# Where the causal mask of a prompt's attention scores is added: by TensorE products or by VectorE

## The chip, the cores and the metric

The kernel runs on one core of a Trainium2 chip. A core has TensorE (PE, matrix products into PSUM), VectorE (DVE), ScalarE (ACT), GpSimd (POOL), and SyncE (SP), which here only issues DMAs. The metric is the device time of one execution in microseconds (us); lower is better. Three executions before the change took 427.47, 427.66 and 428.17 us.

## The reference

One layer of a decoder is computed for a prompt of 256 tokens and for 8 sequences of 4 new tokens each (288 tokens in all, model width 1024). An input projection gives two groups of mixers. One is a gated spatial mixer (4 groups of 128 channels). The other is attention with 8 heads of 64: the new tokens attend to a paged cache of 1024 old tokens by blocks, and the prompt attends to itself, causally, inside one block of 256 keys. Then come an output projection, an MLP of width 4096 and a gated per-layer embedding. What matters here is the prompt's attention:

```python
mask = slot_ok[None, None, :, :, None] & (pos <= t[None, None, :, None, None])
s = jnp.einsum('bhqd,bhqnkd->bhqnk', q, kg).astype(jnp.float32) * (d ** -0.5)
s = jnp.where(mask, s, -jnp.inf)
p = jax.nn.softmax(s.reshape(b, h, nq, -1), axis=-1)
```

## The kernel before

Activations lie with features on the partitions and 288 tokens along the free axis. Weights are streamed in 104 chunks of 512 KB: a DMA on SP's queue brings `raw`, ACT writes its rounded half `hi` (L132), DVE the rest `lo` (L139), and every product is three passes on TensorE (L221, L222, L223). Cached pages of 256 KB come in 16 tiles of 8 pages (`kvt`, four buffers, L160), eight tiles of keys and eight of values; they are asked for on the queues of SP, POOL and ACT.

The first part of the program follows the string `ORDER`: `w` is a chunk of weights, `T` a tile of pages (`u_K`, products at L543; `u_V`, L615), `G` a group of the spatial mixer (`u_g`, L458, L460), `A` a pair of heads of the prompt's attention (`u_A`), `P` the load of the embedding's input (`load_p`, L310). There are four `A`. Units are generators, so that a later part of a unit runs some turns later, after other work. The order of an engine's queue is not simply that of the text: the framework puts the instructions of each engine in order by its own estimates of when each can run, apart from those kept in program order. After this part come the MLP's 64 chunks and the gate's 8.

`u_A(j)` for one pair of heads works in this order. Scores of each head go into one PSUM bank of the ring `misc` (3 banks), for the first 128 queries against 128 keys and for the second 128 against 256 keys (L480; the two heads use rows 0 to 63 and 64 to 127 of the array). To each of the four blocks on the diagonal, a product of an identity with a mask of 0 and -1e30 is added in PSUM (L483). DVE then takes the row maxima from PSUM (L494, L495) and scales them (L496). ACT takes Exp from PSUM into `P` with the row sums (L498, L500). DVE inverts the sums (L503) and scales `P` (L505, L506). TensorE transposes `P` through a third bank (L516), ACT and DVE copy the result to SBUF (L520, L518), TensorE multiplies with the values (L527), and the result is split into two halves (L227, L228). The identity and the mask of the products are a rounded copy `mask_r` of two 128x128 blocks of `const`, made once by ACT (L667).

Of the kernel before, what the change touches and what calls it, by code (L numbers as in the profile page):

```python
# [8 lines left out]
F32R = mybir.dt.float32r  # L9
I32 = mybir.dt.int32  # L10
AF = mybir.ActivationFunctionType
OP = mybir.AluOpType
AX = mybir.AxisListType
# [6 lines left out]
SCALE = 0.125  # L20
NEG = -1e30
# [14 lines left out]

# w: next chunk of weights, T: next tile of cached pages, G: group of the spatial gate, A: head pair of the prompt's
# attention, m: masks, P: input of the layer embedding, s and S: stores, -: a turn without matrix products of its own
ORDER = (
# [6 lines left out]
def tile_decode_step(ctx: ExitStack, tc: tile.TileContext, w, xT, pT, kT, vP, pt, vec, const, aws, abd, abs_,  # L46
                     y_o, k_o, vp_o, vs_o, s_o):
    nc = tc.nc
    pe, act, dve, pool, sp = nc.tensor, nc.scalar, nc.vector, nc.gpsimd, nc.sync
# [5 lines left out]
    def stile(shape, tag, bufs=1, dt=F32):  # L55
        uid[0] += 1
        return sb.tile(shape, dt, name=f"{tag}_{uid[0]}", tag=tag, bufs=bufs)
# [16 lines left out]

# [1 line left out]
    pt_sb = stile([1, 64], "pt", dt=I32)  # L76
    vec_sb = stile([128, 38], "vec")
    cst = stile([128, 476], "const")
    aws_sb = stile([128, 4, 128], "aws")
# [3 lines left out]
    eps = stile([128, 1], "eps")  # L83
# [4 lines left out]
    first = stile([128, 1], "first")  # L88
# [10 lines left out]
    ident = cst[:, 0:128]  # L99
    cmask = cst[:, 128:256]  # L100
    blk = cst[:, 256:384]
    omask = cst[:, 384:448]
    hmask = cst[:, 448:456]
    sel = cst[:, 456:472]
    iota = cst[:, 472:476]

# [1 line left out]
    h = stile([128, 8, N], "h")  # L108
# [5 lines left out]

# [1 line left out]
    NW = w.shape[0]  # L116
# [25 lines left out]

    # pages are asked for at the pace of the arithmetic, so that weights don't queue behind them
    pace = {"pe": 0.0, "dma": 0.0, "page": 0, "used": 0, "w": 6, "split": 2, "wn": 0}
# [18 lines left out]

# [1 line left out]
    pending = []  # L165
# [14 lines left out]
    def step(unit=None, weights=None, us=2.95):  # L180
        """One turn of the pipeline. A generator that yields n goes on n turns later, with those that read PSUM;
        n + 0.5: with those that need PE, after them; 0: at the end of this turn."""
        if weights is not None:
            pace["wn"] = weights
            for c in range(pace["split"], weights + 1):
                load_w(c)
                split_hi(c)
                split_lo(c)
                pace["split"] = c + 1
        ahead = [c for c in range(pace["split"], pace["wn"] + 3) if c in raw]  # L190
        for c in ahead:
            split_hi(c)
            pace["split"] = c + 1
        for q in pending:
            q[0] = max(q[0] - 1, 0)
        due(0)
        due(1)
        if unit is not None:
            resume(unit)
        for c in ahead:  # L200
            split_lo(c)
        # the second half of w_out waits for the last page
        for c in range(pace["w"], pace["split"] + NRAW):
            if c in raw or c >= NW:
                pace["w"] = c + 1
            elif c < W_HOLD or pace["page"] >= PAGE_HOLD:
                load_w(c)
                pace["w"] = c + 1
                pace["dma"] += 1.46
            else:  # L210
                break
        load_pages(us)
        due(2)
# [4 lines left out]

# [1 line left out]
    def mm3(out, wh, wl, xh, xl, start, stop):  # L220
# [17 lines left out]
    def rsqrt_act(ss, count):  # L238
        """first guess of 1/sqrt(ss/count + eps), its square, and -(ss/count + eps)/2"""
        y, v, y2 = tmp(), tmp(), tmp()  # L240
        act.activation(y, ss, AF.Abs_reciprocal_sqrt, bias=eps, scale=1.0 / count)
        act.activation(v, ss, AF.Identity, bias=heps, scale=-0.5 / count)
        act.activation(y2, y, AF.Square)
        return y, v, y2
# [19 lines left out]

# [1 line left out]
    def load_x(i):  # L266
# [38 lines left out]

# [1 line left out]
    def load_p():  # L307
# [55 lines left out]

# [1 line left out]
    def in_tile(c, name, tag):  # L365
# [27 lines left out]
    def nat(src, dst_p, dst_s):  # L393
        """src [128 feat, 288 tokens] -> dst_p [128 tokens, 2, 128 feat], dst_s [32 tokens, 128 feat]"""
        p = misc_ps()
        for c in range(2):
            pe.transpose(p[:, 128 * c:128 * c + 128], src[:, 128 * c:128 * c + 128], ident)  # L397
        pe.transpose(p[0:NS, 256:384], src[:, NP:N], ident)
        act.activation(dst_p, p[:, 0:256].rearrange("p (c f) -> p c f", c=2), AF.Copy)
        act.activation(dst_s, p[0:NS, 256:384], AF.Copy)  # L400
# [51 lines left out]

# [1 line left out]
    def u_g(g):  # L454
# [17 lines left out]

# [1 line left out]
    def u_A(j):  # L474
        qn, kn = st["q"], st["k"]
        S = [misc_ps(), misc_ps()]
        for q0, c0, n in ((0, 0, 128), (128, 256, 256)):
            for hh in range(2):
                pp = slice(64 * hh, 64 * hh + 64)
                pe.matmul(S[hh][:, c0:c0 + n], lhsT=qn[pp, j, q0:q0 + 128], rhs=kn[pp, j, 0:n], start=True, stop=False,  # L480
                          tile_position=(64 * hh, 0))
            for hh in range(2):
                pe.matmul(S[hh][:, c0 + n - 128:c0 + n], lhsT=mask_r[:, 0:128], rhs=mask_r[:, 128:256],  # L483
                          start=False, stop=True)
        yield 1
# [7 lines left out]
        for hh in range(2):  # L493
            dve.tensor_reduce(mx[:, 2 * hh:2 * hh + 1], S[hh][:, 0:128], AX.X, OP.max)  # L494
            dve.tensor_reduce(mx[:, 2 * hh + 1:2 * hh + 2], S[hh][:, 256:512], AX.X, OP.max)  # L495
        dve.tensor_scalar(mx, mx, -SCALE, None, op0=OP.mult)  # L496
        for hh in range(2):
            act.activation(P[hh][:, 0:128], S[hh][:, 0:128], AF.Exp, bias=mx[:, 2 * hh:2 * hh + 1], scale=SCALE,  # L498
                           accum_out=sm[:, 2 * hh:2 * hh + 1])
            act.activation(P[hh][:, 128:384], S[hh][:, 256:512], AF.Exp, bias=mx[:, 2 * hh + 1:2 * hh + 2],  # L500
                           scale=SCALE, accum_out=sm[:, 2 * hh + 1:2 * hh + 2])
# [29 lines left out]

# [1 line left out]
    def u_K(t):  # L533
# [98 lines left out]

# [1 line left out]
    def u_out(c, half, i):  # L634
# [27 lines left out]

# [1 line left out]
    mask_r = stile([128, 256], "maskr", dt=F32R)  # L664

    def mask_aws():
        act.activation(mask_r, cst[:, 0:256], AF.Copy)  # L667
        tc.keep_in_program_order(pool.dma_start(aws_sb, aws))
        tc.keep_in_program_order(pool.dma_start(abd_sb, abd))
        tc.keep_in_program_order(pool.dma_start(abs_sb, abs_.partition_broadcast(128)))  # L670
        pool.affine_select(out=aws_sb, in_=aws_sb, pattern=[[0, 4], [1, 128]], compare_op=OP.is_ge, fill=0.0, base=0,
                           channel_multiplier=-1)
        pool.affine_select(out=abd_sb, in_=abd_sb, pattern=[[0, 4], [1, NS]], compare_op=OP.is_ge, fill=0.0, base=0,
                           channel_multiplier=-1)
# [36 lines left out]

# [1 line left out]
    hid = []  # L713
# [3 lines left out]
    for nm in ("T5", "T6"):  # L717
        t = stile([128, 4 * N], nm)
# [74 lines left out]
def _constants():  # L793
    import numpy as np
    c = np.zeros((128, 476), np.float32)
    i = np.arange(128)
    c[:, 0:128] = np.eye(128)
    c[:, 128:256] = np.where(i[None, :] <= i[:, None], 0.0, NEG)
    c[:, 256:384] = (i[:, None] // 64 == i[None, :] // 64)
    b4, q = i // 32, (i % 32) // 8  # L800
    for g in range(2):
        key = np.arange(32)
        ok = (key[None, :] // 4 == (4 * g + b4)[:, None]) & (key[None, :] % 4 <= q[:, None])
        c[:, 384 + 32 * g:416 + 32 * g] = np.where(ok, 0.0, NEG)
    c[:, 448:456] = (i[:, None] % 8 == np.arange(8)[None, :])
    c[:, 456:472] = (i[:, None] // 8 == np.arange(16)[None, :])
    c[:, 472:476] = np.arange(1, 5)[None, :]
    return c
# [56 lines left out]
```

## Time and profile before

| | before |
|---|---|
| time, three executions | 427.47, 427.66, 428.17 us |
| profiled execution: span from first to last instruction | 425.1 us |
| what lies around the span, if the profiled execution took the median | 2.6 us |
| TensorE busy | 414.2 us (97%) |
| VectorE busy | 270.0 us (64%) |
| ScalarE busy | 206.9 us (49%) |
| mean granted TensorE clock, share of full | 0.995 |

Busy time of TensorE counts each product to its modelled end, and these ends overlap the next product, so 97% does not say that the array streams all the time. The chain that ended last, followed back from the last instruction, says which engine's work the end waited for.

### The profile page before, as it was taken

To read this page: it belongs to the slowest core of one execution; us is meant where nothing else is said; L and a number is where in the kernel's file an instruction comes from. 1 tells how busy PE (TensorE), PEld (TensorE's weight loads), DVE (VectorE), ACT (ScalarE), POOL (GpSimd) and SP (SyncE) were. 2 spreads that over 40 slices of the span, in tenths; PEclk is the share of its full clock that TensorE was granted. 3 is DMA by queue.
4 is the path that set the end of the run, shared out by engine and by line. 5 is a ranking of instruction groups with operands and counts; after the bars stand their busy time and mean duration, and the time that the engine had idled before them with its cause. 6 is when DMAs were issued, how large, how long until landed. Compare 5 with 4: busy or idle time off the path is not lost.

```text
span 425.1 us, 8557 instructions
## 1 busy us (share of the span) xinstructions
PE 414.2 (97%) x3100; PEld 371.2 (87%) x3100; DVE 270.0 (64%) x485; ACT 206.9 (49%) x370; POOL 41.5 (10%) x65
## 2 busy tenths in 40 slices
PE   5999999999999999998999999999999999999995
PEld 4997869893575584998999999999999999999995
DVE  4788434657546563597999978777435445435773
ACT  6587325767252353666555445444333343343631
POOL 5401211103113220041000000000000000000000
PEclk9899999999999999999999999999999999999999
DMA  8999994888899688943454545445445455455411
GB/s 269 323 307 351 395 392 158 284 294 306 295 310 311 219 283 310 324 161 126 172 170 154 173 155 188 154 159 188 150 166 180 150 168 178 147 183 167 159 47 56
DMA packets 33963, 92.29 MB, mean 217 GB/s; under 512 B 4753, under 2 KB 6049, under 8 KB 33921
## 3 DMA queue, kind: packets, MB, share of 16 engines
q1 hardware_dynamic: 28944, 77.52, 52.6%
q0 software_dynamic: 3824, 12.34, 8.1%
q10 hardware_dynamic: 1152, 1.89, 1.3%
q8 instruction: 24, 0.39, 0.4%
q14 instruction: 19, 0.15, 0.1%
HBM read 89.31 MB, written 2.42 MB: 216 GB/s over the span
## 4 chain that ended last, share of the span: by engine, by line
PE 93%; DVE 3%; DMA 1%; issue 1%; ACT 1%; SPq 0%; DVEq 0%
PE mm L221 24%; PE mm L222 24%; PE mm L223 24%; PE S L543 5%; PE S L615 4%; PE misc L235 2%; PE misc L480 1%; DMA h<-xT 1%; PE misc L527 1%; DVE T L231 1%; DVE lo L139 1%; PE misc L516 1%; PE misc L483 1%; PE misc L397 1%; PE misc L458 1%
## 5 line engine op out<-in xcount | busy, mean ns | idle before, releaser
L132 ACT ACTIVATE hi<-raw 128x1024 fp32r<-128x1024 f32 (+1 forms) x104 | 108.4, 1043 | 131.2 <-PE mm L222 104.1
L139 DVE TENSOR_TENSOR lo<-raw,hi 128x1024 fp32r<-128x1024 f32 (+1 forms) x104 | 125.0, 1202 | 59.9 <-ACT hi L132 58.2
L221 PE MATMUL mm<-T,hi 128*128 128x288 f32 x296 | 87.9, 298 | 0.2 <-ACT T L230 0.2
L222 PE MATMUL mm<-T,hi 128*128 128x288 f32 x296 | 86.7, 293 | 1.2 <-DVE T L231 1.2
L221 PE MATMUL mm<-Ah,hi 128*128 128x288 f32 x280 | 85.9, 307 | 1.5 <-ACT Ah L230 0.8
L223 PE MATMUL mm<-T,lo 128*128 128x288 f32 x296 | 86.8, 294 | 0.0
L222 PE MATMUL mm<-Al,hi 128*128 128x288 f32 x280 | 84.8, 303 | 1.9 <-DVE Al L231 1.9
L223 PE MATMUL mm<-Ah,lo 128*128 128x288 f32 x280 | 83.6, 299 | 0.4 <-DVE lo L139 0.4
L221 PE MATMUL mm<-kv,hi 128*128 128x288 f32 x224 | 66.1, 295 | 0.0
L222 PE MATMUL mm<-kv,hi 128*128 128x288 f32 x224 | 66.0, 295 | 0.0
L223 PE MATMUL mm<-kv,lo 128*128 128x288 f32 x224 | 65.9, 294 | 0.0
L222 PEld LDWEIGHTS mm<-Al,hi 128*128 128x128 f32 x280 | 53.3, 190 | 5.7 <-issue 3.1
L221 PEld LDWEIGHTS mm<-Ah,hi 128*128 128x128 f32 x280 | 53.1, 190 | 5.2 <-issue 2.9
L222 PEld LDWEIGHTS mm<-T,hi 128*128 128x128 f32 x296 | 55.6, 188 | 1.6 <-DVE T L231 1.5
L221 PEld LDWEIGHTS mm<-T,hi 128*128 128x128 f32 x296 | 55.5, 188 | 0.5 <-ACT T L230 0.4
L223 PEld LDWEIGHTS mm<-T,lo 128*128 128x128 f32 x296 | 55.4, 187 | 0.0
L223 PEld LDWEIGHTS mm<-Ah,lo 128*128 128x128 f32 x280 | 53.3, 190 | 1.7 <-issue 1.0
L222 PEld LDWEIGHTS mm<-kv,hi 128*128 128x128 f32 x224 | 42.3, 189 | 0.0
L223 PEld LDWEIGHTS mm<-kv,lo 128*128 128x128 f32 x224 | 42.3, 189 | 0.0
L221 PEld LDWEIGHTS mm<-kv,hi 128*128 128x128 f32 x224 | 42.0, 188 | 0.0
L543 PE MATMUL S<-kv,T 128*32 128x256 f32 x256 | 24.3, 384 | 0.0
L736 DVE TENSOR_TENSOR tmp<-mm,rs 128x288 f32<-128x288 f32 x32 | 14.6, 456 | 10.8 <-PE mm L223 10.7
(193 smaller groups left out, 446.8 us busy)
## 6 DMA issues: line engine op xcount, KB each, us to landing
raw<-w SPq DMA_DIRECT2D x100, 512.0 KB, 3.3
kv<-kT SPq DMA_DIRECT2D x46, 256.0 KB, 4.8
kv<-vP SPq DMA_DIRECT2D x31, 256.0 KB, 4.5
kv<-vP POOLq DMA_DIRECT2D x27, 256.0 KB, 5.5
kv<-kT POOLq DMA_DIRECT2D x18, 256.0 KB, 5.5
kv<-vP ACTq DMA_DIRECT2D x6, 256.0 KB, 5.2
h<-xT SPq DMA_DIRECT2D x4, 288.0 KB, 5.2
raw<-w SPq DMA_DIRECT2D x4, 256.0 KB, 5.3
```

Of the source, the lines that this page charges most:

```text
L132: act.activation(hi[c][:, a:b], raw[c][:, a:b], AF.Copy)
L139: dve.tensor_tensor(lo[c][:, a:b], raw[c][:, a:b], hi[c][:, a:b].bitcast(F32), OP.subtract)
L221: pe.matmul(out, lhsT=wh, rhs=xh, start=start, stop=False)
L222: pe.matmul(out, lhsT=wh, rhs=xl, start=False, stop=False)
L223: pe.matmul(out, lhsT=wl, rhs=xh, start=False, stop=stop)
L231: dve.scalar_tensor_tensor(dl, src, scale, dh.bitcast(F32), OP.mult, OP.subtract)
L235: pe.matmul(p[:, :N], lhsT=lhsT, rhs=src, start=True, stop=True)
L397: pe.transpose(p[:, 128 * c:128 * c + 128], src[:, 128 * c:128 * c + 128], ident)
L458: pe.matmul(p[:, 128 * c:128 * c + 128], lhsT=an[:, 128 * c:128 * c + 128], rhs=aws_sb[:, g, :], start=True, stop=True)
L543: pe.matmul(S[32 * b:32 * b + 32, c0:c0 + 256].rearrange("p (j s) -> p j s", j=2), lhsT=Qbd[:, q0:q0 + 32], rhs=kt[:, b, :, j, :], start=j ...
L615: pe.matmul(O[32 * b:32 * b + 32, :], lhsT=PT[:, c:c + 32], rhs=vt[:, v0:v0 + 512], start=False, stop=n == 3 and j == 1, tile_position=(0, ...
L736: dve.tensor_tensor(t, p, st["r2"], OP.mult)
```

## The change

The products with the mask and `mask_r` are gone. The block of `const` that holds the mask is now 256 wide: 128 columns of zero, then the mask's 128. One VectorE instruction per block reads the scores from PSUM and the mask from SBUF, writes their sum to `P` in SBUF and the maxima of its rows to `mx`. Exp reads `P` and writes it in place.

```diff
-    cst = stile([128, 476], "const")
+    cst = stile([128, 604], "const")
...
-    cmask = cst[:, 128:256]
+    cmask = cst[:, 128:384]
...
-                pe.matmul(S[hh][:, c0:c0 + n], lhsT=qn[pp, j, q0:q0 + 128], rhs=kn[pp, j, 0:n], start=True, stop=False,
+                pe.matmul(S[hh][:, c0:c0 + n], lhsT=qn[pp, j, q0:q0 + 128], rhs=kn[pp, j, 0:n], start=True, stop=True,
                           tile_position=(64 * hh, 0))
-            for hh in range(2):
-                pe.matmul(S[hh][:, c0 + n - 128:c0 + n], lhsT=mask_r[:, 0:128], rhs=mask_r[:, 128:256],
-                          start=False, stop=True)
...
         for hh in range(2):
-            dve.tensor_reduce(mx[:, 2 * hh:2 * hh + 1], S[hh][:, 0:128], AX.X, OP.max)
-            dve.tensor_reduce(mx[:, 2 * hh + 1:2 * hh + 2], S[hh][:, 256:512], AX.X, OP.max)
+            for i, (a, b) in enumerate(((0, 128), (256, 512))):
+                dve.tensor_tensor_reduce(P[hh][:, 128 * i:128 * i + b - a], S[hh][:, a:b], cmask[:, 256 - b + a:], 1.0,
+                                         -3e38, OP.add, OP.max, mx[:, 2 * hh + i:2 * hh + i + 1])
         dve.tensor_scalar(mx, mx, -SCALE, None, op0=OP.mult)
         for hh in range(2):
-            act.activation(P[hh][:, 0:128], S[hh][:, 0:128], AF.Exp, bias=mx[:, 2 * hh:2 * hh + 1], scale=SCALE,
+            act.activation(P[hh][:, 0:128], P[hh][:, 0:128], AF.Exp, bias=mx[:, 2 * hh:2 * hh + 1], scale=SCALE,
                            accum_out=sm[:, 2 * hh:2 * hh + 1])
-            act.activation(P[hh][:, 128:384], S[hh][:, 256:512], AF.Exp, bias=mx[:, 2 * hh + 1:2 * hh + 2],
+            act.activation(P[hh][:, 128:384], P[hh][:, 128:384], AF.Exp, bias=mx[:, 2 * hh + 1:2 * hh + 2],
...
-    mask_r = stile([128, 256], "maskr", dt=F32R)
 
     def mask_aws():
-        act.activation(mask_r, cst[:, 0:256], AF.Copy)
```

The other columns of `const` move up by 128, and some comments are dropped.

## Rows read from the trace of the kernel before

**Rows 1.** The page, parts 1 and 2: busy time and share of the span; the DMA engines' busy share in 40 slices of 10.6 us, in tenths.
```profile
PE 414.2 (97%) x3100; PEld 371.2 (87%) x3100; DVE 270.0 (64%) x485; ACT 206.9 (49%) x370; POOL 41.5 (10%) x65
DMA  8999994888899688943454545445445455455411
```

**Rows 2.** The page, part 4: the chain that ended last, share of the span by engine.
```profile
PE 93%; DVE 3%; DMA 1%; issue 1%; ACT 1%; SPq 0%; DVEq 0%
```

**Rows 3.** Busy time by stretch: the second and third pair of heads, and most of the MLP. Columns: stretch and its length, busy us (and count) of PE, PEld, DVE, ACT, POOL, granted clock, DMA share, GB/s.
```profile
125.00:135.00 10.00, 10.00 (x95) 6.16 (x91) 5.52 (x16) 3.28 (x11) 2.35 (x5) 1.00 0.86 294
200.00:420.00 220.00, 220.00 (x1660) 219.70 (x1659) 147.11 (x225) 98.94 (x136) 0.00 (x0) 1.00 0.46 158
```

**Rows 4.** The chain in order of time, 110 to 150 us: start, us, what, and how many instructions (an L480 product is two of them). In this order: pair 0, pair 1, pair 2, pair 3's two pieces with the mask.
```profile
112.61 0.41 PE misc L480 x2
113.02 0.26 PE misc L483
113.28 0.41 PE misc L480 x2
113.69 0.26 PE misc L483
113.95 0.63 PE misc L480 x4
114.58 0.37 PE misc L483 x2
...
128.43 0.42 PE misc L480 x4
128.85 0.37 PE misc L483 x2
129.22 0.63 PE misc L480 x4
129.85 0.37 PE misc L483 x2
...
130.78 0.42 PE misc L480 x2
131.19 0.26 PE misc L483
131.45 0.63 PE misc L480 x2
132.08 1.84 PE S L543 x26
133.92 0.41 PE misc L480 x2
134.34 0.26 PE misc L483
134.59 0.63 PE misc L480 x2
...
135.77 0.37 PE misc L483 x2
...
144.96 0.37 PE misc L483 x2
...
145.96 0.37 PE misc L483 x2
```

**Rows 5.** Groups of instructions by line and shape: count, busy us, mean ns of one, idle before. Two row maxima, an addition that reads PSUM and SBUF, ACT's read-out of a row sum, and two of ACT's instructions, one that reads SBUF and one that reads PSUM.
```profile
L494 DVE TENSOR_REDUCE pmx<-misc 128x1 f32<-128x128 f32 x8 | 2.3, 287 | 2.7 <-PE misc L483 2.7
L495 DVE TENSOR_REDUCE pmx<-misc 128x1 f32<-128x256 f32 x8 | 3.3, 415 | 0.0
L464 DVE TENSOR_TENSOR tmp<-misc,abs 128x256 f32<-128x256 f32 x4 | 1.7, 422 | 3.6 <-PE misc L460 3.6
L498 ACT ACTIVATION_READ_ACCUMULATOR T<-misc,pmx 128x1 f32 x4 | 0.8, 199 | 0.0
L660 ACT ACTIVATE tmp<-h 128x288 f32<-128x288 f32 x14 | 6.0, 428 | 0.0
L227 ACT ACTIVATE Ah<-misc 128x256 fp32r<-128x256 f32 x4 | 1.5, 386 | 7.7 <-PE misc L527 4.5 <-DMA kv<-vP 3.2
```

**Rows 6.** Instructions in order of time, pair 3: start, us, engine, line; idle before and what ended it in brackets. The first row maximum, the first scaling of `P`, the first transpose.
```profile
146.26 0.29 DVE L494 TENSOR_REDUCE pmx<-misc 128x1 f32<-128x128 f32 x1 [1.12 <-PE misc L483]
...
150.25 0.29 DVE L505 TENSOR_SCALAR T<-T,psm 128x128 f32<-128x128 f32 x1
...
150.75 0.27 PE L516 MATMUL misc<-const,T 128*128 128x128 f32 x1
```

**Rows 7.** The waits of SP's own queue between 100 and 175 us: us in total, times, longest. `pT` is the embedding's input, L160 a page.
```profile
SPq L160 <- DMA T<-pT: 4.2, 1, 4.2
```

**Rows 8.** Instructions in order of time at the end of the pages: the load of the embedding's input, the first weight chunk behind the pages as ACT splits it, and the first product that needs its `lo`.
```profile
151.91 0.34 ACTq L310 DMA_DIRECT2D T<-pT  x1
...
165.81 1.06 ACT L132 ACTIVATE hi<-raw 128x1024 fp32r<-128x1024 f32 x1 [6.66 <-DMA raw<-w]
...
168.21 0.36 PE L223 MATMUL misc<-T,lo 128*128 128x288 f32 x1
```

**Rows 9.** ACT in order of time near the start: the copy of the identity and mask, and what follows it.
```profile
15.62 0.40 ACT L667 ACTIVATE maskr<-const 128x256 fp32r<-128x256 f32 x1
17.71 1.06 ACT L132 ACTIVATE hi<-raw 128x1024 fp32r<-128x1024 f32 x1 [1.69 <-PE S L222]
```

More of the change, by code (lines that the diff above doesn't have):

```diff
@@ L99, in tile_decode_step @@
     ident = cst[:, 0:128]
-    cmask = cst[:, 128:256]
[L101 to L105, printed above, removed]
+    cmask = cst[:, 128:384]
+    blk = cst[:, 384:512]
+    omask = cst[:, 512:576]
+    hmask = cst[:, 576:584]
+    sel = cst[:, 584:600]
+    iota = cst[:, 600:604]
     h = stile([128, 8, N], "h")
@@ L794, in _constants @@
     import numpy as np
-    c = np.zeros((128, 476), np.float32)
+    c = np.zeros((128, 604), np.float32)
     i = np.arange(128)
     c[:, 0:128] = np.eye(128)
-    c[:, 128:256] = np.where(i[None, :] <= i[:, None], 0.0, NEG)
-    c[:, 256:384] = (i[:, None] // 64 == i[None, :] // 64)
+    c[:, 256:384] = np.where(i[None, :] <= i[:, None], 0.0, NEG)
+    c[:, 384:512] = (i[:, None] // 64 == i[None, :] // 64)
     b4, q = i // 32, (i % 32) // 8
@@ L803, in _constants @@
         ok = (key[None, :] // 4 == (4 * g + b4)[:, None]) & (key[None, :] % 4 <= q[:, None])
[L804 to L807, printed above, removed]
+        c[:, 512 + 32 * g:544 + 32 * g] = np.where(ok, 0.0, NEG)
+    c[:, 576:584] = (i[:, None] % 8 == np.arange(8)[None, :])
+    c[:, 584:600] = (i[:, None] // 8 == np.arange(16)[None, :])
+    c[:, 600:604] = np.arange(1, 5)[None, :]
     return c
```

## The prediction

> **What bounds the kernel now.** I read the chain that ended last first, because it says whose work the end waits for: 93% of the span is TensorE, 3% VectorE [rows 2]. The reader is to see that nearly every step of the chain leads from one TensorE instruction to the one before it. Busy shares alone would not show that, since the DMA engines are also at 0.8 or 0.9 through the first two fifths of the span [rows 1]. [...] So time taken out of TensorE's queue in the attention should reach the end, unless something that feeds TensorE stays where it is. Last I read the chain in order of time through the four pairs, since that gives what a mask product takes out of TensorE's queue, where busy time would count overlapping ends [rows 4].
>
> **What is removed from TensorE.** The sixteen mask products stand in the chain with 0.26 + 0.26 + 0.37 = 0.89 us in pair 0, 0.37 + 0.37 = 0.74 in pair 1, 0.26 + 0.26 + 0.37 = 0.89 in pair 2 and 0.74 in pair 3 [rows 4]. That is 3.26 us, and it is the least that goes.
>
> More may go, because a mask group interrupts the scores. In pair 1 four records of 128 columns take 0.42 us and four of 256 columns take 0.63. The 0.21 between them is the streaming of 4 x 128 columns, so 0.21 of the first 0.42 is streaming too and the other 0.21 is the entry into a new group [rows 4]. If the second group of scores follows the first directly, that entry falls away: 0.21 in pair 1, and by the same shape 0.21 in pair 3. In pair 0 the second 0.41 becomes two records of about 0.05, which saves 0.31, and the third group saves 0.21: 0.52. In pair 2 each 0.63 for two records of 256 columns becomes 0.21, twice 0.42: 0.84. Together 1.78 us, so the bounds for TensorE are 3.26 and 5.04. The order of the queue is the planner's, and in pair 2 it split the scores around other work (1.84 us of L543 between them). I take three quarters of the 1.78, giving 3.26 + 1.34 = 4.6 us.
>
> **What is added on VectorE.** The row maxima go: 287 ns for 128 columns, 415 for 256. The fused instruction has no row. An addition that reads 256 columns of PSUM and as many of SBUF takes 422 ns, 7 more than the maximum over the same columns [rows 5], so the second operand is close to free. What is left is the write-out of the maxima. From below it costs nothing beyond the 7 ns; from above, ACT's separate read-out of a row sum takes 199 ns [rows 5]. I take the middle, 0.1 us each, 0.4 us per pair. The far upper bound is two passes per element as well: 128 more columns cost 415 - 287 = 0.128 us, so a pair would pay 2 x 0.128 + 2 x 0.256 = 0.77, and with four read-outs 0.8 more, 1.57 us. VectorE has room for any of these as an engine (5.52 us of 10 busy).
>
> [...]
>
> **Where this lies on the path.** In pair 3 VectorE begins its maxima at 146.26, ends the first scaling of `P` at 150.54, and the first transpose starts at 150.75 [rows 6]. That is 4.3 us of VectorE and ACT with 0.2 us to spare, covered by products of other units. The next thing that waits if this gets longer is TensorE itself, at the transposes, with all products queued behind them. So I charge pair 3 the whole 0.4 us. In pairs 1 and 2 the planner has other products to put between (26 L543 products of 1.84 us stand inside pair 2); I charge half, 0.2 each, and pair 0 nothing. Total 0.8 us. With the far bound of 1.57 it would be 1.57 x 2 = 3.1.
>
> **What costs nothing.** Exp now reads SBUF. A copy of 288 columns from SBUF takes 428 ns, one of 256 from PSUM 386 [rows 5]; even if all 42 ns were the source's and not the 32 columns', a pair's four Exps pay 0.17 us, and ACT is busy 3.28 us of 10 there. The banks of the scores come free after VectorE's reading instead of after Exp, which can only help the next user of the ring; I count no gain, since TensorE is not seen waiting for a bank in the rows. The copy to `mask_r` took 0.40 us of ACT, just before 1.69 us in which ACT waited for TensorE [rows 9]: no gain. The DMA of `const` carries 128 x 128 x 4 = 65.5 KB more, 0.22 us at 294 GB/s [rows 3]; the weight chunks queue behind it, and the same 1.69 us hide that. Uncovered it would cost 0.2.
>
> **The end of the pages.** This is the place where a gain could vanish. The first weight chunk behind the pages is split by ACT at 165.81, after ACT had waited 6.66 us for its DMA; the product that needs its `lo` starts at 168.21, about as soon as 1.06 us of ACT and VectorE's part allow [rows 8]. There is no slack: if that DMA does not come earlier, TensorE waits for it. It should come earlier. SP's last pages, in front of that chunk, wait 4.2 us for the landing of `pT` [rows 7], and ACT issues `pT` at 151.91, behind pair 3's transposes [rows 8]. So this chain is itself set off by TensorE's progress, and the DMA engines had room in the slices before (a 6 among the 8s and 9s [rows 1]). I let it move along in full.
>
> **The sum.** 4.6 - 0.8 = 3.8 us. The profiled span of 425.1 becomes 421.3. What lies around it, 2.6 us, is the same, so 427.66 becomes 423.9 us. The span and the median of the three executions belong together if the profiled execution was a typical one; the three differ by 0.7 us. About 0.2%, 0.86 us, is what a measurement of this kernel can tell from no change.
>
> **The rivals.**
> *Pair latency eats half.* The read-outs cost 0.2 us or more, or the planner leaves the transposes where they are, so that TensorE waits in three pairs. For: the 0.2 us of spare in pair 3. Against: the scores end earlier by as much as is removed. Gain 0.9 to 2.4 us: 425.2 to 426.8 us.
> *The transfers do not move.* If the pages from 140 to 166 us are paced by the DMA engines and not by TensorE's releases, TensorE arrives 4 us early at the chunk of 165.81 and waits. For: no slack there, and DMA digits of 8 and 9. Against: the chain through `pT`. Time 426.8 to 428: the same.
> *The fused instruction is the new bound: slower.* Place: between scores and transposes of all four pairs. Price: 1.57 us per pair without any cover, 6.3 in all against 4.6, that is 429.4 us. It decides from 4.6 / 16 = 0.29 us more per instruction than the maximum took, uncovered. For: nothing in the rows shows this instruction. Against: 422 ns for the addition. [...]
> *The planner's new order is worse: slower.* Each group of products torn apart pays an entry of 0.2 to 0.4 us [rows 4]; it takes some 15 more of these to turn 3.8 us around. 428.5 to 430 us.
> *The change does not do what it says* cannot be for the sixteen products themselves; that only the 3.26 us go is inside my forecast.
>
> **How the numbers follow.** Forecast (gain 2.4 to 5.3, 422.4 to 425.2): 0.57. Latency eats half: 0.20. Transfers do not move: 0.12. Fused instruction: 0.06. Order: 0.05. Faster is then 0.77, same 0.12, slower 0.11. The range 422.4 to 427.5 leaves out the two slower cases and about half of the same, 0.17.
>
> **What would show it.** Right: no L483; scores of a pair in one or two groups with about 0.84 us in all; the fused rows at 0.3 and 0.42 us, a read-out below 0.2; the chain still TensorE through the transposes; the first chunk behind the pages split some 4 us earlier, at about 162; the later stretches merely moved. Wrong: TensorE's waits on VectorE at the transposes; the wait of ACT for that chunk longer than 6.66 us with its DMA landing where it did; fused rows of 0.6 us; many more short groups of L543 or L480.

## The result and the profile after

The kernel became slower: 431.4 us median against 428.4 for the kernel before beside it, ratio 1.0066 with a 95% interval of 1.0038 to 1.0094. That lies outside the range of the prediction and on the other side of its forecast. The profiled execution took 430.29 us with a span of 428.7.

Page of the kernel after, parts 1, 2 and 4: busy time, the DMA engines in 40 slices, the chain by engine.
```profile
PE 417.9 (97%) x3084; PEld 371.3 (87%) x3084; DVE 269.9 (63%) x501; ACT 206.7 (48%) x369; POOL 40.2 (9%) x65
DMA  8999984888996679943454544544545445445411
PE 93%; DVE 3%; DMA 1%; ACT 1%; issue 1%; SPq 0%; DVEq 0%
```
TensorE has sixteen instructions fewer and is busy 3.7 us longer than in [rows 1]. The chain is its own as before [rows 2]. So nothing took TensorE's place as the bound; it needs more time for less work.

Kernel after, groups by line and shape between 90 and 160 us: the fused instruction and its read-out.
```profile
L492 DVE CUSTOM_DVE_ANT_0 PP<-misc,const 128x256 f32<-128x256 f32 x4 | 1.7, 420 | 0.0
L492 DVE DVE_READ_ACCUMULATOR2_ANT pmx<- 128x1 f32 x16 | 1.3, 83 | 0.0
L492 DVE CUSTOM_DVE_ANT_0 PP<-misc,const 128x128 f32<-128x128 f32 x4 | 1.2, 289 | 0.2 <-PE misc L480 0.2
```
The new instruction takes 289 and 420 ns where the row maximum took 287 and 415 [rows 5], and its read-out 83 ns. It is as cheap as the prediction had it.

Kernel after, the chain in order of time: start, us, what, number of instructions. The scores, and the products of the cached K pages (L541; before L543) and V pages (L613; before L615) between and around them.
```profile
115.27 0.98 PE S L613 x4
116.25 0.33 PE mm L221
116.58 0.13 PE mm L222
116.71 1.83 PE S L613 x10
...
128.97 1.84 PE S L541 x26
130.81 1.50 PE misc L480 x12
132.32 0.56 PE S L541 x6
132.88 0.85 PE misc L480 x4
...
142.65 0.85 PE misc L480 x4
143.50 1.84 PE S L541 x26
145.34 0.85 PE misc L480 x4
...
160.70 0.57 PE misc L590 x4
...
162.22 0.69 DVE PT L592
...
162.99 0.19 DVE PT L597
...
163.22 1.06 PE S L606 x8
164.28 7.00 PE S L613 x64
```
The masks are gone and the scores are short. But this is not the queue of [rows 4] with the masks taken out: pairs 1 and 2 follow each other in one group of twelve, seven products of V pages stand in two pieces with two chunk products between, and at 162.2 TensorE waits for VectorE ahead of the last sums over the V pages.

Kernel after, this wait among those of TensorE (us in total, times, longest).
```profile
PE S L606 <- DVE PT L597: 0.9, 1, 0.9
```

Kernel after, ACT in order of time: the first weight chunk behind the pages.
```profile
168.87 1.06 ACT L132 ACTIVATE hi<-raw 128x1024 fp32r<-128x1024 f32 x1 [6.39 <-DMA raw<-w]
```
It starts 3.06 us later than in [rows 8], not 4 earlier.

To see where time goes, the start of ACT's split of a chunk (L132) is subtracted from that of the same chunk before. The first column below is what the start of the execution gave or cost, and it differs between executions; the others are read against it. A split can run ahead of TensorE (e12 at 165.8), so the end is read from the last two columns. The kernels e1 to e12 are explained below.

```
delay against before, us, of the chunk that ACT splits before at (us)
                          24.6   72.3   74.8   97.5  126.1  165.8  193.7  384.8
after                    -0.22  -0.17  +0.57  +0.57  +1.97  +3.06  +3.58  +3.56
e1 edit, old order       -0.35  -0.35  -0.35  -0.35  -1.41  -4.33  -4.02  -4.30
e2 masks, new order      -0.80  -0.75  -0.01  -0.01  +1.64  +4.06 +11.09 +11.35
e3 no mask, old order    +0.53  +0.53  +0.53  +0.53  -0.56  -2.00  -1.71  -1.74
e4 no mask, own order    +1.12  +1.12  +1.12  +1.12  +2.52  +4.30  +4.61  +4.33
e5 new order first       +0.85  +0.90  +1.64  +1.64  +0.57  -2.18  -1.88  -1.90
e6 new order pairs 1-3   -0.31  -0.31  -0.31  -0.31  -1.37  -0.34  +1.52  +1.24
e7 new order pair 0      +0.20  +0.20  +0.20  +0.20  +1.60  -1.07  -0.63  -0.91
e8 whole pieces          -0.82  -0.82  -0.82  -0.82  -2.94  -7.14  -6.69  -6.69
e9 Exp from PSUM         -0.37  -0.37  -0.37  -0.37  -1.46  -5.29  -3.98  -4.26
e10 e3, wide constants   -0.27  -0.27  -0.27  -0.27  -1.32  -4.33  -3.84  -3.87
e11 one tear             +0.42  +0.42  +0.42  +0.42  +0.51  -3.99  -2.14  -2.17
e12 fused twice          -0.16  -0.16  -0.16  -0.16  -1.13  -8.12  -1.72  -1.72
```
The kernel after loses 0.74 us at 72 to 75 us, long before the first fused instruction at 114.1, then 1.4 by 126, 1.1 by 166 and 0.5 by 194. The MLP behind is only moved. A loss where the edit has no instruction points to the order of the queues: the framework's planner orders each engine's instructions by its own estimates, and it wrote TensorE's, ACT's and VectorE's queues anew, TensorE's from place 218 of the 2799 in its queue on. SP's and POOL's queues kept theirs.

### The profile page after: what moved, and what is told of

Read it like the earlier page. It is cut to its first block, busy times and chain, and to the rows that moved or that the text cites. A ratio compares the mean times of both kernels' runs of the same rounds, so it can differ in the third digit from the quotient of the medians.

```text
span 428.7 us, 8536 instructions
## 1 busy us (share of the span) xinstructions
PE 417.9 (97%) x3084; PEld 371.3 (87%) x3084; DVE 269.9 (63%) x501; ACT 206.7 (48%) x369; POOL 40.2 (9%) x65
## 4 chain that ended last, share of the span: by engine, by line
PE 93%; DVE 3%; DMA 1%; ACT 1%; issue 1%; SPq 0%; DVEq 0%
PE mm L221 24%; PE mm L223 24%; PE mm L222 24%; PE S L541 6%; PE S L613 4%; PE misc L235 2%; PE misc L525 1%; DMA h<-xT 1%; PE misc L480 1%; DVE T L231 1%; DVE lo L139 1%; PE misc L514 1%; PE misc L458 1%; PE misc L397 1%; PE misc L590 1%
## 5 line engine op out<-in xcount | busy, mean ns | idle before, releaser
L132 ACT ACTIVATE hi<-raw 128x1024 fp32r<-128x1024 f32 (+1 forms) x104 | 108.4, 1042 | 130.2 <-PE mm L222 103.3
L541 PE MATMUL S<-kv,T 128*32 128x256 f32 x256 | 26.7, 384 | 0.0
L731 DVE TENSOR_TENSOR tmp<-mm,rs 128x288 f32<-128x288 f32 x32 | 14.6, 457 | 10.8 <-PE mm L223 10.6
```

What stands on the lines that cost most here:

```text
L132: act.activation(hi[c][:, a:b], raw[c][:, a:b], AF.Copy)
L541: pe.matmul(S[32 * b:32 * b + 32, c0:c0 + 256].rearrange("p (j s) -> p j s", j=2), lhsT=Qbd[:, q0:q0 + 32], rhs=kt[:, b, :, j, :], start=j ...
L731: dve.tensor_tensor(t, p, st["r2"], OP.mult)
```

## The experiments

**The two orders crossed.** The theory is that the edit is worth what was predicted and the planner's new order loses more. To part the two, a table of places is added to a kernel, by which each engine issues; edges between neighbours fix the order (TensorE in e1, which is ordered so, waits 0.2 us in all between 97 and 175 us).

```diff
+def pin_order(tc, nc):
+    orders = json.loads(zlib.decompress(base64.b85decode(QUEUE_ORDER)))
+    ins = list(nc.cur_bb.bb.instructions)
+    for name, order in orders.items():
+        mine = [i for i in ins if str(i.engine) == "EngineType." + name
+                and type(i).__name__ not in ("InstRegisterAlu", "BassTilePoolBoundary")]
+        for a, b in zip(order, order[1:]):
+            tc.add_manual_dep(mine[b], mine[a].name, ...)
...
         tile_decode_step(tc, *args)
+        pin_order(tc, nc)
```

*e1*: the kernel after, with the order of the kernel before.

> The changed kernel (mask added by the fused VectorE instruction, no mask products), but every engine issues its instructions in the order in which the kernel before issued them (the sixteen mask products and the copy of the mask simply missing). Theory 'order': the loss comes from the order that the planner wrote anew, so here the working of the prediction holds: 4.6 us of products gone, 0.4 to 0.8 given back by the pairs, 423.5 to 425 us against 427.7, ratio 0.990 to 0.994. Rival 'pair latency or instruction': the loss hangs on the fused instruction and on what waits for it, whatever the order: 430 to 432 us, ratio 1.004 to 1.009. Rival 'transfers': the stretch of the pages is set by page transfers that do not move: 427 to 428.5 us, ratio 0.998 to 1.002.

Measured: 422.5 us, ratio 0.9908 [0.9886, 0.9930]. The same instructions as in the kernel after, 3.9 us faster than before instead of 2.8 slower (the ratios of 427.66). Kernels are compared by these ratios to the kernel before beside them, and their intervals matter below.

*e2*: the kernel before, with the order of the kernel after.

> The kernel before, mask products and plain row maxima and all, but every engine issues in the order of the changed kernel; the mask products stand right behind their scores, which follow one another as they do there. Theory 'order': slower than before by what the order costs, some 3.6 us of the changed kernel's trace plus the 3.8 us that the edit was to save, so 434 to 436 us if the two add up, and in no case under 430; ratio 1.006 to 1.02. Rivals 'pair latency or instruction' and 'transfers': the order is worth nothing, 427 to 429 us, ratio 0.998 to 1.003.

Measured: 438.0 us, ratio 1.0255 [1.0235, 1.0275]. The new order makes the old arithmetic slower too, but by 10.9 us, more than the 6.8 us by which it costs the edited kernel (1.0066 - 0.9908 of 427.66) and above the 434 to 436 us expected. The two do not simply add. Two things show in the trace of e2: Exp still holds the banks of the scores, so TensorE waits for it among the pairs, and in two stretches, each behind a wait, the granted clock is lower.

e2, the two longest waits of TensorE between 126 and 200 us, and busy time by stretch (columns as in [rows 3]).
```profile
PE misc L480 <- ACT T L500: 0.9, 1, 0.9
PE S L608 <- DVE PT L599: 0.9, 1, 0.9
```
```profile
120.00:150.00 30.00, 28.93 (x201) 16.87 (x200) 13.59 (x42) 7.23 (x26) 4.33 (x8) 0.94 0.63 212
166.00:174.00 8.00, 7.08 (x43) 2.61 (x45) 3.73 (x7) 4.67 (x13) 0.00 (x0) 0.79 1.00 368
```
The 64 records of V products behind the second wait take 8.70 us in its chain, against 7.00 in the kernel after, whose granted clock stays at 1.00 there; 0.79 is e2's mean over 166 to 174 us. That the wait brings the lower clock is not shown: the kernel after has the same wait of 0.9 us ahead of the same products and keeps 1.00. How the 10.9 us divide was not worked out.

*e3*: no mask at all (so the prompt's attention is not causal), order of before; *e4*: the same kernel in the order that the planner writes for it. The edit of both:
```diff
-                pe.matmul(S[hh][:, c0:c0 + n], lhsT=qn[pp, j, q0:q0 + 128], rhs=kn[pp, j, 0:n], start=True, stop=False,
+                pe.matmul(S[hh][:, c0:c0 + n], lhsT=qn[pp, j, q0:q0 + 128], rhs=kn[pp, j, 0:n], start=True, stop=True,
                           tile_position=(64 * hh, 0))
-            for hh in range(2):
-                pe.matmul(S[hh][:, c0 + n - 128:c0 + n], lhsT=mask_r[:, 0:128], rhs=mask_r[:, 128:256],
-                          start=False, stop=True)
...
-        act.activation(mask_r, cst[:, 0:256], AF.Copy)
```


> The kernel before with the mask left out altogether: no mask products, plain row maxima from PSUM, Exp from PSUM, so the prompt's attention is not causal; order of issue as before on every engine. It prices the removal alone. Theory 'order': 4.6 us less than before, 422.5 to 424 us, ratio 0.988 to 0.992, and at most 0.8 us under the edit in the old order: that difference is the price of the fused instruction with its read-out. Rival 'instruction': this kernel is fast (423) while the edit in the old order is not (430 or more). Rival 'transfers': 427 to 428.5.

> The same work as the kernel without any mask, but in the order that the planner writes for it by itself, a third order (it parts from the kernel before at the first missing mask product). Theory 'order': a time of its own, anywhere from 422 to 432 us, that differs from the same work in the old order by more than 1 us. Rival 'instruction': the same 423 us as in the old order, since no fused instruction is in it.

Measured: e3 424.0 us, ratio 0.9924 [0.9907, 0.9941]; e4 429.7 us, ratio 1.0058 [1.0038, 1.0078]. With no fused instruction in it and work only taken away, the planner's own order makes the kernel slower than before, by 5.7 us against the same work in the old order. That rules out the rivals that need the fused instruction. The surprise is e3 against e1: leaving the mask out came out slower than adding it on VectorE, by 1.4 us in the medians and 0.7 in the ratios. The intervals of the two ratios overlap, so this may be scatter. It is taken up below.

**Where in the order the time is lost.** TensorE's two orders are permutations of each other within short stretches, so the new one can be put back stretch by stretch into e1. e5 has it ahead of the prompt's attention, e7 around pair 0, e6 from pairs 1 and 2 on:
```diff
-    QUEUE_ORDER = old order
+    e5: new order in PE[0:641], ACT[0:140], DVE[0:133], old order elsewhere
+    e7: new order in PE[641:723], DVE[133:159], old order elsewhere
+    e6: new order in PE[723:], ACT[140:], DVE[159:], old order elsewhere
```


> The edit in the old order, with the changed kernel's order put back only ahead of the prompt's attention (before about 111 us). Theory 'the planner's order, added up by stretches': the changed kernel's trace falls 0.74 us behind the edit in the old order there, between 72 and 75 us, so 423 to 424 us, ratio 0.991 to 0.995. If the whole loss were begun there (pages that come late and stay late), 428 to 431 us.

> The edit in the old order, with the changed kernel's order put back only around pair 0 (from its scores to the first scores of pair 1, about 112 to 128 us). Theory 'by stretches': the changed kernel's trace loses 2.46 us between 97 and 126 us, so 424.5 to 426 us, ratio 0.994 to 0.9985. Otherwise 422 to 423.5 us.

> The edit in the old order, with the changed kernel's order put back only from the second half of pair 1 and pair 2 on (from about 129 us: pairs 1 to 3, the last tile of pages, the sums of the pages). Theory 'by stretches': the changed kernel's trace loses 4.0 us here up to 166 us and 0.5 after it, so 426 to 428 us, ratio 0.998 to 1.003. If order matters only through when the first page products or pair 0 come, 422 to 423.5 us, ratio 0.989 to 0.992.

Measured: e5 423.2 us, 0.9913 [0.9891, 0.9935]; e7 425.5 us, 0.9967 [0.9953, 0.9981]; e6 427.5 us, 1.0001 [0.9987, 1.0016]. Each lies where the stretch in the kernel after's own trace put it. Over e1 the ratios come to 0.2, 2.5 and 4.0 us, together 6.7 of the 6.8 that the whole order costs. (The single profiled executions, by the last column of the table less the first, give 1.2, 2.8 and 5.5 against 7.7, so the sum holds within an execution's scatter of a microsecond or two.) No run pins a kernel to the order that it has anyway. But e5, e6 and e7 are pinned like e1 and the kernel after is not, so a sum of 6.7 against 6.8 leaves little for the pinning itself.

**What a piece of page products costs.** The next theory is the mechanism: a group of page products torn in two pays for it. e11 makes one tear in e1, the one seen above at 115.27. e8 goes the other way: the K-page products between 117 and 145 us in 5 pieces instead of e1's 12.
```diff
 order of TensorE, from place 648
-    7 x L613, L221, L222
+    2 x L613, L221, L222, 5 x L613                                             (e11)
```
```diff
 order of TensorE, from place 673: the L541 groups (chunk products fill the places that come free)
-    2, 1, 2, 11, 3, 13 of the first tile; 1, 1, 1, 13, 1, 15 of the second
+    3, 16, 13          of the first tile; 16, 16             of the second      (e8)
```


> The edit in the old order, with a single change of order: two chunk products stand within the first group of seven page products behind pair 0, as in the changed kernel, so that one piece becomes two. Theory 'a torn group pays its entry': in the two traces the pieces of four and ten took 0.98 and 1.83 us against 1.84 for the piece of fourteen (each product shows as two), and one more chunk product took 0.33 instead of 0.13, so 1.0 to 1.2 us more than the edit in the old order: 423.5 to 423.8 us, ratio 0.993 to 0.9945. Otherwise, if only waits cost: 422.5 us, ratio 0.9905 to 0.9915.

> The edit in the old order, but the products of the cached K pages that TensorE meets between about 117 and 145 us stand in 5 pieces instead of 12 (the seven small ones joined to the next long one, chunk products put in their places). Theory 'a torn group pays its entry': a piece of two takes 0.55 us where two products within a long piece take 0.14, and the chunk product behind a piece takes 0.33 instead of 0.13, so about 0.6 us for a piece that is gone and 4.2 us for seven, if nothing waits in their place; some of it will come back as waits of the transposes and at the last page transfers, so 419 to 422 us, ratio 0.982 to 0.989. Rival 'small pieces cost nothing, they only fill waits': 422.5 us or more, ratio 0.990 or more.

Measured: e11 424.6 us, 0.9932 [0.9907, 0.9956]; by the ratios 1.0 us more than e1 (the intervals overlap; 2.1 by the medians), and by the delays between 72.3 and 126.1 (+0.09 against -1.06) 1.15. The trace shows it more firmly than the time: one tear, one microsecond. e8 420.5 us, 0.9848 [0.9825, 0.9872]: 2.6 us less than e1 by the ratios (2.0 by the medians), the fastest of all, and faster than both kernels.

e11, its chain around the tear:
```profile
115.12 0.98 PE S L613 x4
116.10 0.33 PE mm L221
116.43 0.13 PE mm L222
116.56 1.83 PE S L613 x10
```
e1, the same products in one piece, and pieces of K products in its chain:
```profile
114.35 1.84 PE S L613 x14
116.19 0.33 PE mm L221
...
120.20 0.55 PE S L541 x2
...
122.54 0.56 PE S L541 x4
...
125.58 1.43 PE S L541 x22
...
129.55 1.84 PE S L541 x26
...
142.84 1.86 PE S L541 x30
```
Two records take as long as four (0.55, 0.56), thirty as long as twenty-six (1.86, 1.84), and four and ten V records together 2.81 where fourteen take 1.84. Time goes up in steps of eight records, about 0.43 us a step for K and 0.85 for V, plus some 0.1 for the entry (an estimate: 0.56 and 0.98 less a step). (One piece of six records took 0.82 us in e1 where its like took 0.56 in the kernel after; that is not explained.) So a tear costs a further started step, and the chunk product behind it shows 0.33 instead of 0.13.

The 0.74 us that the kernel after loses at 72 to 75 us are such a tear too. There the new order puts two chunk products into a piece of six K records, and e5 shows it alone.

e5, its chain around 70 us:
```profile
70.02 0.55 PE S L541 x2
70.56 0.33 PE mm L221
70.90 0.13 PE mm L222
71.02 0.56 PE S L541 x4
```
e1, the same products in one piece:
```profile
69.02 0.56 PE S L541 x6
```
The two pieces take 1.11 us instead of 0.56 and the first chunk product 0.33 instead of 0.13, together 0.75; e5 loses 0.74 between 72.3 and 74.8 in the table.

The groups of L541 between 90 and 175 us in e1, after and e8 (12, 15 and 5 pieces), one line from each:
```profile
L541 PE MATMUL S<-kv,T 128*32 128x256 f32 x128 | 12.4, 384 | 0.0
```
```profile
L541 PE MATMUL S<-kv,T 128*32 128x256 f32 x128 | 14.1, 385 | 0.0
```
```profile
L541 PE MATMUL S<-kv,T 128*32 128x256 f32 x128 | 9.2, 383 | 0.8 <-DVE bm L557 0.8
```
The same 128 records are busy between 9.2 and 14.1 us: (14.1 - 12.4) / 3 = 0.57 us a piece from e1 to after, (12.4 - 9.2) / 7 = 0.46 from e8 to e1. e8 was to save up to 4.2 us and saved 2.6; 0.8 of the rest is the new wait in its line, for VectorE's maxima over the page scores.

**The fused instruction, Exp and the start.** e12 issues each fused instruction twice; e9 lets Exp read PSUM again, so that the mask reaches the maxima only; e10 is e3 with the constants laid out as in the kernel after.
```diff
-                dve.tensor_tensor_reduce(P[hh][:, 128 * i:128 * i + b - a], S[hh][:, a:b], ...)
+                for _ in range(2):                                                            # e12
+                    dve.tensor_tensor_reduce(P[hh][:, 128 * i:128 * i + b - a], S[hh][:, a:b], ...)
```
```diff
-            act.activation(P[hh][:, 0:128], P[hh][:, 0:128], AF.Exp, ...
+            act.activation(P[hh][:, 0:128], S[hh][:, 0:128], AF.Exp, ...                      # e9
```
```diff
-    cst = stile([128, 476], "const")
+    cst = stile([128, 604], "const")                                                          # e10
```


> The edit in the old order, with every fused instruction issued twice, one behind the other: 2 x 0.290 + 2 x 0.420 + 4 x 0.083 = 1.75 us more on VectorE for each pair. The prediction charged what VectorE adds to pair 3 in full, to pairs 1 and 2 by half and to pair 0 not at all; by that 1.75 x (1 + 0.5 + 0.5) = 3.5 us more than the edit in the old order, 426 us, ratio 0.9975 to 1.0005. Theory 'pair latency' of the prediction's first rival charges each pair in full: 7.0 us, 429.5 us, ratio 1.005 to 1.009. If the work between covers it, 422.5 to 424 us, ratio 0.9905 to 0.994.

> The edit in the old order, but Exp reads the scores from PSUM, as the kernel before does, so the mask reaches the maxima only and the attention is not causal; the fused instruction still writes its masked scores, which nobody reads. The edit in the old order ran 1.4 us faster than the kernel without any mask in the same order. Theory 'banks': Exp from SBUF sets the PSUM banks free sooner, which is worth that 1.4 us, so about 424 us here, ratio 0.992 to 0.9945. Theory 'start and transfers': that difference comes from before the prompt's attention (the first 18 us) and from the last transfers, so 422 to 423 us here, ratio 0.989 to 0.9915.

> The kernel without any mask in the old order, with the constants laid out in 604 columns as in the changed kernel instead of 476; nothing else is different from the kernel without any mask. Theory 'start': the wider load of constants moves the start, so 422 to 423 us, ratio 0.989 to 0.9915. Theory 'banks': as the kernel without any mask, 423.5 to 424.5 us, ratio 0.9915 to 0.9945.

Measured: e12 425.1 us, 0.9946 [0.9918, 0.9974]; e9 423.1 us, 0.9895 [0.9856, 0.9934]; e10 422.8 us, 0.9886 [0.9846, 0.9925]. Doubling costs 1.6 us by the ratios, 2.6 by the medians and 2.4 in the profiled execution, between the two cases named: less than the 3.5 of the prediction's charges, more than full cover. TensorE's waits say where:

e12, the waits of TensorE between 97 and 175 us (in this kernel L515 is the transposes and L504 the scaling of `P`):
```profile
PE misc L515 <- DVE T L504: 1.9, 2, 1.2
```
Both stand at the transposes of the pairs whose `P` is the tile `T`, 1 and 3. So the prediction's place for a late pair was right, and its weights were not: pairs 1 and 3, pair 2 hidden.

By the ratios Exp from PSUM (e9) is no slower than e1, so what lies between e3 and e1 is not the banks. e10 is e3 but for the width of the constants, and it is no slower than e1 either; but its interval overlaps e3's, so that the width does it isn't shown. Two things differ between the profiled executions. The first is the start: at 24.6 us e3 is at +0.53, e1 at -0.35 and e10 at -0.27.

Busy time of the first 18 us, e3 and then e10 (columns as in [rows 3]):
```profile
0.00:18.00 18.00, 14.56 (x65) 13.34 (x66) 12.02 (x21) 10.43 (x18) 9.81 (x14) 0.81 0.88 306
```
```profile
0.00:18.00 18.00, 15.42 (x71) 13.77 (x72) 12.10 (x21) 11.12 (x19) 9.23 (x14) 1.00 0.88 306
```
The granted clock is 0.81 in one and 1.00 in the other, with 65 and 71 products done. e1, with the wide constants, had 0.81 as well, so the width does not set the clock, and the clock does not sort the starts. The second is at the end of the pages, where TensorE in e3 stands for the first weight chunk behind them; e1 and e10 have no such wait.

e3, the waits of TensorE for that chunk, between 97 and 200 us, and two pieces of the chain that leads to them: the load of `pT` and that of the chunk.
```profile
PE misc L223 <- DVE lo L139: 0.7, 1, 0.7
PE misc L221 <- ACT hi L132: 0.3, 1, 0.3
```
```profile
148.62 7.14 DMA T<-pT
...
157.45 6.34 DMA raw<-w
```
The start gives 0.9 and this wait 1.0 of the 2.6 us between the profiled executions of e3 and e1 (425.02 and 422.45). Whether the other executions of e3 had that wait isn't on record, and why these loads took so long there stays open.

## Why the prediction was wrong, point by point

**What bounds the kernel** was read rightly: the chain is TensorE's at 93% before, after and in e1, and time taken out of its queue reaches the end (e1, 3.9 us). In e3 it is 89%, with 4% of DMA, since that chain runs through `pT` and the late chunk. The 5.52 us of VectorE and 3.28 of ACT in 10 that the prediction counts as room belong to the stretch of 125 to 135 us [rows 3].

**The removed products.** From each record's start to the next one's, in the stretch of the attention and the last pages:
```
us, start to next start    before      e1   after
scores L480                  5.65    4.64    5.20
mask products                3.05       -       -
K pages                     11.40   11.58   13.02
V pages                      8.99    8.99    9.82
transposes of the sums       0.57    0.57    2.68
PV L525 / L527               3.93    3.93    4.49
```
In the old order 3.05 + 1.01 = 4.06 us go, against 4.6 taken from bounds of 3.26 and 5.04. That the entries are saved was right; 1.01 of the 1.78 came, not three quarters. The mask products themselves are 3.05 from start to start, under the 3.26 called the least.

**VectorE's part.** The write-out of the maxima stands in the trace of the kernel after as an instruction of its own: sixteen reads are there. At 83 ns they are under the 199 of ACT's [rows 5].

e1, VectorE in pair 3: the four fused instructions.
```profile
142.07 0.29 DVE L492 CUSTOM_DVE_ANT_0 T<-misc,const 128x128 f32<-128x128 f32 x1 [0.29 <-PE misc L480]
142.29 0.08 DVE L492 DVE_READ_ACCUMULATOR2_ANT pmx<- 128x1 f32 x1
142.29 0.42 DVE L492 CUSTOM_DVE_ANT_0 T<-misc,const 128x256 f32<-128x256 f32 x1
...
142.85 0.42 DVE L492 CUSTOM_DVE_ANT_0 T<-misc,const 128x256 f32<-128x256 f32 x1
143.19 0.08 DVE L492 DVE_READ_ACCUMULATOR2_ANT pmx<- 128x1 f32 x1
```
From the first to the end of the last read it is 1.20 us. Before, the maxima of pair 3 began at 146.26 [rows 6] and the last of them ended at 147.40: 1.14.

Before, VectorE in pair 3: the last maximum.
```profile
146.99 0.41 DVE L495 TENSOR_REDUCE pmx<-misc 128x1 f32<-128x256 f32 x1
```
A pair pays 0.06 us and not 0.4, since the read starts together with the next instruction (both at 142.29). The far bound's second pass over each element is not there either: 420 ns for 256 columns is no double of the maximum's 415 [rows 5]. The rival of the slow instruction falls with it.

**What costs nothing.** Exp from SBUF, the banks and the copy: by the ratios e9 and e1 are the same, so right within what is measured.

**The end of the pages** moved along in e1, as forecast: the first chunk behind them is split at 161.48, 4.33 us earlier than in [rows 8], and TensorE does not wait for it. So the rival that the transfers stay falls for e1; in the profiled execution of e3 it came true in part, with the 1.0 us above. After, `pT` is issued at 153.44, 1.5 us later than before, and the chunk is split 3.06 later. The argued way through `pT` is there in e3's chain, but `pT` does not always set the chunk: in e12 it is issued at 150.25, 2.6 us later than in e1 (147.63), and the chunk is split 3.8 us earlier.

**The sum.** 4.06 less what VectorE costs is within 0.2 of the predicted 3.8; e1 measured 0.9908, which of 427.66 is 423.7 us, and the prediction said 423.9. That it is so close is in part luck: 0.5 us less came off TensorE than was charged, and some 0.7 less was added by VectorE (0.06 for the 0.4 of a pair), and the two errors cancel. The 2.6 us taken to lie around the span do not fit either: every execution with both figures on record has 1.5 to 1.7. The forecast does not change by it, since the same 2.6 stands on both sides. The working holds in the main for a kernel whose queues keep their order. The chip did not get that kernel.

**The step that failed** is the one that took the queue for the old one with holes in it. "The order of the queue is the planner's" stands in the prediction, but only to weigh the entries of the scores. Everything else was moved rigidly, and the rival of the new order got 0.05. Two errors made that chance small. First, a tear was priced at 0.2 to 0.4 us, the entry read between score groups, where page products pay a started step: about 0.5 us in K's group and 0.2 behind it (e5, together 0.74), 1.0 for V (e11). At some 0.6 us each, "some 15 more" should have been about six for 3.8 us. Second, waits were left out: after, the transposes of the sums stretch from 0.57 us to 2.68, 2.1 us of one late step. By the table, the kernel after pays over e1 2.1 there, 1.44 for three more pieces of K, 0.83 for a torn V group, 0.56 for scores and 0.56 for PV; the first part adds 0.74. That is 6.2 of the 7.7 us between the two profiled executions, less the start. The tears of page products are tested by themselves (e5, e11, e8). The late step of the sums, the scores and PV are read from the trace, and no run puts them back alone. The list of signs for "wrong" did name more short groups of L543.

What in the edit sets off the planner isn't shown in full. Taking the products away is enough (e4), and that order parts from the old one only at the first missing mask product. The parting from place 218 on must come from the rest of the edit, since e4 lacks it; which part was not tried.

## What to carry to other kernels

Where a planner orders the queues, an edit is two changes: the instructions, and an order of everything else that can cost more than they gain (here 6.8 us against 3.9). Measure the edit with the old order pinned before judging it, and read the new order on its own: count the pieces of the groups that pay by steps, and look for TensorE's new waits. Here the edit with the old order is worth 0.9%, and with whole pieces (e8) 1.5%.

## What the chip showed that was not expected

- Products on 32 columns of weights go by started steps of eight records, that is of four products: two records 0.55 us and four 0.56, twenty-six 1.84 and thirty 1.86 (K); four 0.98, ten 1.83, fourteen 1.84 (V). The kernel puts four in a row on columns 0, 32, 64 and 96 of the array, and the trace of the kernel after shows them starting together: the first four records of the piece of 26 at 128.90 to 128.92 us, the next four at 129.14 to 129.16, four more at 129.35 to 129.37.
- VectorE's accumulator read (82 to 86 ns in the kernel after) starts with the next fused instruction and hides behind it: in e1's pair 3 the maxima with four reads of 0.08 us take 0.06 us longer than before without them.
- In e2 a wait of 0.9 us without a product was followed by a granted clock of 0.79 over 166 to 174 us, with 8.70 us for products that take 7.00 in the kernel after. There the same wait was followed by 1.00, so what made the difference stays open.
- The first 18 us ran at a granted clock of 0.81, 0.91 or 1.00 from one profiled execution to another, and the start moved all that followed by up to 1.9 us (from -0.82 to +1.12 at 24.6). The two do not go together: at 0.81 e3 stood at +0.53 and e1 at -0.35, at 1.00 e10 at -0.27, and e8, the earliest, had 0.91. What moves the start stays open.
